# Strassen's algorithm, one level, in the down projection of a ConvGLU layer (20 of 22 contraction tiles), with the weight sums formed in HBM by accumulating DMAs

## The chip, the cores and the metric

The kernel runs on one core of one Trainium2 chip. Work is spread over five engines that run side by side, each with its own queue in a fixed order: TensorE (PE) multiplies matrices into PSUM, VectorE (DVE) and ScalarE (ACT) do elementwise work, GpSimd (POOL) sets memory and issues some DMAs, SyncE (SP) issues most DMAs. They wait for one another through semaphores. All DMAs, whichever queue issues them, share 16 DMA engines. The metric is the device time of one execution in microseconds (us), the median of several runs.

## The reference

One layer: a token mixer, then the channel mixer below, for 512 latent tokens (8 rows of 64), model width 1024, and inner width `D_FF` 2816. Everything is float32. Only the last product is touched by the change.

```python
def _conv_ffn(h, rows, w_up, conv_w, conv_b, w_down):
    bsz, length, _ = h.shape
    a, val = _split(h @ w_up, (D_FF, D_FF))
    img = a.reshape(bsz, rows, length // rows, D_FF)
    a = lax.conv_general_dilated(img, conv_w[:, :, None, :], (1, 1), 'SAME',
                                 dimension_numbers=('NHWC', 'HWIO', 'NHWC'),
                                 feature_group_count=D_FF) + conv_b
    return (jax.nn.gelu(a.reshape(bsz, length, D_FF), approximate=False) * val) @ w_down
...
x = x + g2x * _conv_ffn(hx2, rows, ffn_w_up[l], ffn_conv_w[l], ffn_conv_b[l], ffn_w_down[l])
return _rms_norm(x, final_norm_g)
```

The last product is (512 x 2816) by (2816 x 1024); its result is scaled by `g2x`, added to the residual `x`, and normalised.

## The kernel before

**Numbers as pairs.** A float32 operand goes into TensorE as two float32r tiles, a rounded `hi` and the rest `lo`, and each product is three matmuls: hi·hi, hi·lo, lo·hi. For weights, `stream_split` makes the pair: ACT casts `raw` into `wh` (L185) and DVE subtracts (`wl`, L186). For activations `split_act` does the same (L309, L310).

**The stream of weights.** All weight blocks of 512 KB stand in one list, `specs`, in the order of their use. `weights()` hands out block i, has the blocks up to i + 1 split, and has SP issue the loads up to block i + 3 (`AHEAD`). There are four `raw` buffers and five of `wh` and of `wl`; a load waits until the split of four blocks before has read its buffer. Each block serves 24 matmuls of 512 columns in nearly all stages.

**The order of the work.** A scheduler sets the order of each engine's queue from the program's text and its data dependences; `in_order` pins parts of it. DMAs from SP are issued strictly in queue order, so one that waits holds up all behind it.

**The stages that matter here.** (1) Up to about 245 us: the input products and the linear attention. (2) From there to about 480 us: the spatial gate, the two branch products, and beside them, a few steps per weight block (`tick`), `ada2`: the modulation vector is computed on DVE, with 64 multiply-adds into eight `acc` tiles (L1133) over 64 loads of `w_ada` (tiles `wa`, L1132). In two parts of four, an `acc` tile is first set to zero by POOL (`G.memset`, L1124) and its first row loaded from `b_ada` by SP (L1126). (3) The up projection: 22 tiles `f`, two weight blocks each (L317); `conv_part` does for each the 3x3 convolution as nine taps (ACT L1346, DVE L1352 eight times), Gelu (ACT L1353) and the product with the gate (DVE L1354) into `gact`. (4) The down projection: for each half of the 1024 output columns, 22 contraction tiles, four token tiles of 128 (`down`, L1395): 2 x 22 x 4 x 3 = 528 matmuls. The last `TAIL` = 6 contraction tiles are done token tile by token tile, so that `out_step` and `out_tok` (the scale by g2, the residual, the norm, the store; L1403 to L1427) run beside the rest; the very last tile comes in two pieces of 256 columns.

```python
def down(ps, g, w, kk, t, c0, n, first, last):
    gh, gl_ = g
    wh, wl = w
    for i, (a, b) in enumerate(((gh, wh), (gh, wl), (gl_, wh))):
        T.matmul(ps, a[:, t * P:(t + 1) * P], b[:, kk, c0:c0 + n], start=(first and i == 0),
                 stop=(last and i == 2))
```

**POOL's queue** holds, besides some early constants, 11 small DMAs near 31 us (`rest_load`), two memsets of `pmask`, and the two times four memsets of `acc`.

Of the kernel before, what the change touches and what calls it, by code (L numbers as in the profile page):

```python
# [23 lines left out]
FT = 22  # L24
GW = 64
# [2 lines left out]
HEAP = 44  # L28
LATE = 27
AHEAD = 3  # L30


@with_exitstack
def backbone_kernel(
# [7 lines left out]
    V, A, G, T = nc.vector, nc.scalar, nc.gpsimd, nc.tensor  # L42
# [5 lines left out]
    sp = stack.enter_context(tc.tile_pool(name="sp", bufs=8))  # L48
    pm = stack.enter_context(tc.tile_pool(name="pm", bufs=4, space=bass.MemoryType.PSUM))
    pg = stack.enter_context(tc.tile_pool(name="pg", bufs=4, space=bass.MemoryType.PSUM))  # L50

    cnt = [0]
# [25 lines left out]
    def traced():  # L78
        return nc.cur_bb.bb.instructions

    def in_order(start, *engines):

        last = {}
        for i in traced()[start:]:
            e = i.engine
            if e in engines:
                if e in last:
                    tc.add_manual_dep(i, last[e], mybir.DependencyInfo(
                        mybir.DependencyClass.NoSync, mybir.DependencyReason.DATA), reason="in_order")
                last[e] = i.name  # L90
# [12 lines left out]
    eps_t = const([P, 1], "eps_t")  # L103
# [54 lines left out]
    for f in range(FT):  # L158
        w_cols(ffn_w_up[0], f * P)
        w_cols(ffn_w_up[0], FF + f * P)  # L160
    for half in range(2):
        for k in range(FT // 2):
            w_cols(ffn_w_down[0], half * 512, 512, 2 * k, 2)

    raws, splits = {}, {}
    pos = [0, 0, 0]
# [10 lines left out]
    def stream_split(upto):  # L177
        while pos[1] < min(upto, len(specs)):
            i = pos[1]
            stream_load(i + 1)  # L180
            _, kn, n = specs[i]
            raw = raws.pop(i)
            wh = wp.tile([P, kn, n], F32R, tag="wh", name=nm("wh"))
            wl = wp.tile([P, kn, n], F32R, tag="wl", name=nm("wl"))
            A.copy(wh, raw)  # L185
            V.tensor_tensor(wl, raw, wh.bitcast(F32), op=ALU.subtract)  # L186
            splits[i] = (wh, wl)
            pos[1] += 1
# [117 lines left out]
    def split_act(src, n=512, s="a", lo_pool=heap, hi_pool=heap, eng=None):  # L306
        hi = hi_pool([P, n], F32R, s=s + "h")
        lo = lo_pool([P, n], F32R, s=s + "l")
        (eng or V.tensor_copy)(hi, src)  # L309
        V.tensor_tensor(lo, src, hi.bitcast(F32), op=ALU.subtract)  # L310
        return hi, lo
# [358 lines left out]
    dst, aps = ada_dot(1)  # L670
# [12 lines left out]
    for k in range(1, KT):  # L683
        g = max(i for i in range(NG) if G0[i] <= k)
# [6 lines left out]
        for z in range(3):  # L691
            if nxt and z == AT[g]:
                dst, aps = ada_dot(nxt)
# [41 lines left out]
    for d in range(2):  # L735
        t_ = late([P, 4, P], s="pmask")
# [599 lines left out]
    wide_tm(mg, wo_done, hook, {(2, 6): turn_first})  # L1336


    gact = []
# [31 lines left out]
    stream_split(pos[2] + 2)  # L1371
    in_order(N2[0], T.engine, A.engine, V.engine)
    conv_part(0, pss[0], pss[1])
    for f in range(1, FT):
# [19 lines left out]
        for i, (a, b) in enumerate(((gh, wh), (gh, wl), (gl_, wh))):  # L1394
            T.matmul(ps, a[:, t * P:(t + 1) * P], b[:, kk, c0:c0 + n], start=(first and i == 0),  # L1395
                     stop=(last and i == 2))

    TAIL = 6

    def out_add(pv, hf, t, c0, n):  # L1400
        tmp = late([P, n], s="yt")
        xv = x1[t][hf][:, c0:c0 + n]
        V.tensor_tensor(tmp, pv, bc_g["g2", hf][:, c0:c0 + n], op=ALU.mult)  # L1403
        V.tensor_tensor(xv, xv, tmp, op=ALU.add)
        return tmp, xv

    def out_step(pv, hf, t, c0, n, part):
        tmp, xv = out_add(pv, hf, t, c0, n)
        A.activation(tmp, xv, AF.Square, accum_out=ss3[:, t, part:part + 1])

    def out_tok(t, part, before):

        b_, r = small(1, "n3b"), small(1, "n3r")
        start = len(traced())
        part()
        if before > 1:
            V.reduce_sum(b_, ss3[:, t, :before], axis=AX.X)
            V.tensor_scalar(b_, b_, 1.0 / D, EPS, op0=ALU.mult, op1=ALU.add)
        else:
            V.tensor_scalar(b_, ss3[:, t, 0:1], 1.0 / D, EPS, op0=ALU.mult, op1=ALU.add)  # L1420
        A.activation(r, ss3[:, t, before:before + 1], AF.Sqrt, bias=b_, scale=1.0 / D)
# [4 lines left out]
        V.scalar_tensor_tensor(x1[t][1], x1[t][1], r, fng[1], op0=ALU.mult, op1=ALU.mult)  # L1426
        dma(out[0, t * P:(t + 1) * P, 512:1024], x1[t][1])  # L1427

    for hf in range(2):
        pss = [(mm if hf else gl)() for _ in range(4)]  # L1430
        for kc_ in range((FT - TAIL) // 2):
            w = weights()
            for kk in range(2):
                k = 2 * kc_ + kk
                if hf == 0:
                    gs.append(split_act(gact[k].rearrange("p r w -> p (r w)"), s="g"))
                for t in range(4):
                    down(pss[t], gs[k], w, kk, t, 0, 512, k == 0, hf == 1 and t == 3 and k == FT - TAIL - 1)
        wl3 = [weights() for _ in range(TAIL // 2)]
        if hf == 0:  # L1440
            for k in range(FT - TAIL, FT):
                gs.append(split_act(gact[k].rearrange("p r w -> p (r w)"), s="g", lo_pool=late))
        else:

            out_add(pss[3], 1, 3, 0, 512)
        for t in range(4):
            pieces = [(0, 256), (256, 256)] if hf and t == 3 else [(0, 512)]
            for i, (c0, n) in enumerate(pieces):
                ps = gl() if hf and t == 3 else pss[t]
                for k in range(FT - TAIL, FT):  # L1450
                    down(ps[:, :n], gs[k], wl3[(k - FT + TAIL) // 2], k % 2, t, c0, n,
                         hf == 1 and t == 3 and k == FT - TAIL, k == FT - 1)
                step = lambda: out_step(ps[:, :n], hf, t, c0, n, hf + i)
                if hf == 0 or i + 1 < len(pieces):
                    step()
                else:
                    out_tok(t, step, hf + i)
            if hf == 0:
                xg.append(late([P, 512], s="xg"))
                V.tensor_tensor(xg[t], x1[t][0], fng[0], op=ALU.mult)  # L1460


# [28 lines left out]
```

## Time and profile before

| | |
|---|---|
| median of 3 runs | 939.61 us (939.19 to 940.34) |
| span of the profiled execution | 938.1 us |
| busy: PE, DVE, ACT, POOL | 925.1, 647.5, 365.2, 13.4 us |
| granted TensorE clock, mean | 0.999 |
| bytes read from HBM, written | 109.04 MB, 2.10 MB |

How to read the rows quoted below. The page's first part gives busy time, share of the span and number of instructions for each engine. The chain is the work that ended last, followed back from the end. In timelines and in the chain in order of time, a row begins with its start and its duration in us; neighbouring instructions of one kind are one row with their count. Rows of groups by form end in the busy time in us, the mean of one instruction in ns, and the engine's idle time before them. Rows of stretches (A:B) give for each engine the busy time and the number of instructions, then the clock, the share of time that the 16 DMA engines were busy, and GB/s.

### The profile page before, as it was taken

The numbers are of one execution on the slowest core, as the hardware profiler recorded it, in microseconds if no ns is written. First come the engines' busy times: TensorE is split into PE (matmuls) and PEld (weight loads), VectorE is DVE, ScalarE is ACT, GpSimd is POOL, SyncE is SP. The second block draws the span as 40 slices with busy tenths as digits, with TensorE's granted clock in tenths as the row PEclk, the third lists the DMA queues.
The fourth block names the chain that finished last, engine by engine and source line by source line (L and its number), as shares of the span: only waits on it lengthen the run. The fifth ranks groups of instructions, "written<-read, shape, count | busy, mean of one in ns | idle before, by whom it ended". The sixth has DMA issues, their size and how long they took to land.

```text
span 938.1 us, 12079 instructions
## 1 busy us (share of the span) xinstructions
PE 925.1 (99%) x4618; PEld 773.5 (82%) x4618; DVE 647.5 (69%) x1132; ACT 365.2 (39%) x616; POOL 13.4 (1%) x34
## 2 busy tenths in 40 slices
PE   7999999999999999999999999999999999999997
PEld 5778888888888888888888889888888888888886
DVE  5578687688898652596664358977777777893414
ACT  5356465565542232222222247443333334211313
POOL 1200000000000000000000000000000000000000
PEclk9999999999999999999999999999999999999999
DMA  9951400511508553483532521533333332232302
GB/s 283 320 155 41 118 23 1 180 45 46 158 26 250 175 191 99 139 289 107 185 112 90 188 87 53 155 108 90 101 102 90 91 110 92 81 116 73 113 1 90
DMA packets 146215, 111.93 MB, mean 119 GB/s; under 512 B 5945, under 2 KB 121989, under 8 KB 146157
## 3 DMA queue, kind: packets, MB, share of 16 engines
q1 hardware_dynamic: 145117, 109.85, 37.9%
q10 hardware_dynamic: 688, 1.09, 0.3%
q8 instruction: 36, 0.59, 0.2%
q0 software_dynamic: 352, 0.22, 0.1%
q14 instruction: 22, 0.18, 0.1%
HBM read 109.04 MB, written 2.10 MB: 118 GB/s over the span
## 4 chain that ended last, share of the span: by engine, by line
PE 98%; ACT 0%; DMA 0%; DVE 0%; issue 0%; ACTq 0%
PE mm L317 55%; PE mm L335 12%; PE gl L1395 7%; PE mm L1395 6%; PE gl L841 3%; PE mm L611 2%; PE gl L611 1%; PE mm L948 1%; PE mm L998 1%; PE gl L335 1%; PE gl L520 1%; PE gl L876 1%; PE gl L1164 1%; PE mm L484 1%; PE gl L317 1%; PE mm L328 1%
## 5 line engine op out<-in xcount | busy, mean ns | idle before, releaser
L185 ACT CAST wh<-raw 128x1024 fp32r<-128x1024 f32 x139 | 146.0, 1054 | 356.9 <-PE mm L317 220.4
L186 DVE TENSOR_TENSOR wl<-raw,wh 128x1024 fp32r<-128x1024 f32 x139 | 168.8, 1219 | 125.3 <-ACT wh L185 124.8
L317 PE MATMUL mm<-h2l,wh 128*128 128x512 f32 (+1 forms) x344 | 133.0, 387 | 0.0
L317 PE MATMUL mm<-h2h,wh 128*128 128x512 f32 (+1 forms) x344 | 133.0, 387 | 0.0
L317 PE MATMUL mm<-h2h,wl 128*128 128x512 f32 (+1 forms) x344 | 133.0, 387 | 0.0
L1352 DVE SCALAR_TENSOR_TENSOR cacc<-ca,ccol,cacc 128x441 f32<-128x441 f32 (+2 forms) x176 | 121.8, 695 | 4.4 <-ACT cacc L1346 0.2
L317 PE MATMUL mm<-hxh,wh 128*128 128x512 f32 x296 | 116.1, 392 | 0.0
L317 PE MATMUL mm<-hxl,wh 128*128 128x512 f32 x296 | 115.4, 390 | 0.0
L317 PE MATMUL mm<-hxh,wl 128*128 128x512 f32 x296 | 115.4, 390 | 0.0
L317 PEld LDWEIGHTS mm<-h2l,wh 128*128 128x128 f32 x344 | 64.6, 188 | 13.2
L317 PEld LDWEIGHTS mm<-h2h,wh 128*128 128x128 f32 x344 | 64.6, 188 | 13.2
L317 PEld LDWEIGHTS mm<-h2h,wl 128*128 128x128 f32 x344 | 64.6, 188 | 12.9
L317 PEld LDWEIGHTS mm<-hxh,wl 128*128 128x128 f32 x296 | 55.5, 188 | 11.6
L317 PEld LDWEIGHTS mm<-hxh,wh 128*128 128x128 f32 x296 | 55.6, 188 | 11.2
L317 PEld LDWEIGHTS mm<-hxl,wh 128*128 128x128 f32 x296 | 55.6, 188 | 11.2
L1133 DVE SCALAR_TENSOR_TENSOR acc<-wa,cs,acc 128x512 f32<-128x512 f32 x64 | 45.7, 744 | 1.5 <-DMA wa<-in_w_ada_dram 1.5
L1395 PE MATMUL gl<-wl,gh 128*128 128x512 f32 (+1 forms) x100 | 37.6, 376 | 0.0
L1395 PE MATMUL gl<-wh,gl 128*128 128x512 f32 (+1 forms) x100 | 37.6, 376 | 0.0
L1395 PE MATMUL gl<-wh,gh 128*128 128x512 f32 (+1 forms) x100 | 37.6, 376 | 0.0
L1353 ACT ACTIVATE cacc<-cacc 128x512 f32<-128x512 f32 x22 | 13.9, 632 | 56.6 <-DVE cacc L1352 56.6
L335 PE MATMUL mm<-wh,hxh 128*128 128x512 f32 x88 | 34.7, 394 | 0.0
L335 PE MATMUL mm<-wl,hxh 128*128 128x512 f32 x88 | 34.4, 390 | 0.0
(398 smaller groups left out, 1671.6 us busy)
## 6 DMA issues: line engine op xcount, KB each, us to landing
raw<-in_w_in_dram SPq DMA_DIRECT2D x52, 512.0 KB, 3.8
wa<-in_w_ada_dram SPq DMA_DIRECT2D x96, 256.0 KB, 4.6
raw<-in_ffn_w_up_dram SPq DMA_DIRECT2D x44, 512.0 KB, 3.7
raw<-in_ffn_w_down_dram SPq DMA_DIRECT2D x22, 512.0 KB, 3.5
raw<-in_w_br_a_dram SPq DMA_DIRECT2D x8, 512.0 KB, 5.2
raw<-in_w_br_b_dram SPq DMA_DIRECT2D x8, 512.0 KB, 3.9
raw<-in_w_o_dram SPq DMA_DIRECT2D x8, 512.0 KB, 3.6
xin<-in_x_dram SPq DMA_DIRECT2D x8, 256.0 KB, 3.4
```

The lines of the kernel that those rows point to most:

```text
L185: A.copy(wh, raw)
L186: V.tensor_tensor(wl, raw, wh.bitcast(F32), op=ALU.subtract)
L317: T.matmul(ps, a[:, k, :], b[:, c0:c0 + n], start=(k == 0 and i == 0), stop=(k == KT - 1 and i == 2))
L328: T.matmul(ps, a[:, k, :], b[:, c0:c0 + n], start=(k == 0 and i == 0), stop=(k == KT - 1 and i == 2))
L335: T.matmul(ps, a[:, t * P:(t + 1) * P], b[:, k % 2, :], start=(k == 0 and i == 0), stop=(k == KT - 1 and i == 2))
L484: T.matmul(xps[1][:, :256], ones, ident.unsqueeze(1).to_broadcast([P, 2, P]), start=True, stop=True)
L611: T.matmul(fps[i], a, b, start=(k == 0 and z == 0), stop=(k == KT - 1 and z == 2))
L841: T.matmul(ps, p_, q_, start=(start and z == 0), stop=(stop and z == 2))
L1133: V.scalar_tensor_tensor(acc[j], w_, cs[:, k, 0:1], acc[j], op0=ALU.mult, op1=ALU.add)
L1352: V.scalar_tensor_tensor(o, a_[:, r0 + dy:r1 + dy, c0 + dx:c1 + dx], wcol(tap), o, op0=ALU.mult, op1=ALU.add)
L1353: A.activation(acc, acc, AF.Gelu)
L1395: T.matmul(ps, a[:, t * P:(t + 1) * P], b[:, kk, c0:c0 + n], start=(first and i == 0), stop=(last and i == 2))
```

## The change

**The products.** Tiles 0 to 19 of the contraction are taken in five blocks (`BLOCKS`) of four. In each block the activations are a 2 x 2 matrix (token halves of 256, pairs of contraction tiles) and so are the weights (pairs of contraction tiles, output halves of 512). A form of Strassen's scheme with seven products computes the 2 x 2 result. A product over one block is 2 token tiles x 2 contraction tiles x 3 = 12 matmuls; one product over all five blocks adds up in two PSUM banks (`products`). So 7 x 5 x 12 = 420 matmuls stand for 480; tiles 20 and 21 stay as they were (48 matmuls, `rest_in`).

**The results.** DVE joins the seven products with adds and subtracts of 128 x 512 (`combine`, results in `u2`, `w5`, `u4`, `c21`, `e22`), partly out of PSUM; ACT takes the first one out (`taken`). The second output half is partly added to the residual early (`todo`).

**The activations.** `conv_part` writes the product with the gate as two halves of 256 tokens into `gpair`. `all_preps` forms for each of the 35 (product, block) pairs its operand, a quarter or a sum or difference of quarters (`tile_op`, 128 x 512 on DVE), and splits it (`act_both`: ACT `dah`, DVE `dal`). Up to eight (`EARLY`) are made during the up projection, later ones five (`LEAD`) ahead of use.

**The weights.** Four of the seven weight operands are sums of quarters. They are formed in HBM: 20 tiles `sum` of 256 x 512 (rows padded to 576), by 20 plain copies and 20 DMAs that add to what stands there (`accum_op`), all on POOL's queue. One is issued at each call of `weights()` from the third block on; each waits for the instruction that was written last before it. The 40 DMAs span blocks 2 to 41 of the stream. The down projection then takes 37 blocks of 512 KB from the stream instead of 22: 20 of them are `sum` tiles, and each of the 35 product blocks serves 12 matmuls.

**The end.** The order at the end is new: in the second output half, three blocks of the last product, then token tiles 2 and 3 by their rest alone, then for token tiles 0 and 1 the last two blocks and the rest. The last tile is no longer cut in two pieces. A dummy square root on ACT stands ahead of the end.

On POOL's queue the eight memsets of `acc` used to follow the memsets of `pmask` directly (before):

```order
L737 MEMSET pmask_951 128x512
L1124 MEMSET acc_2913 128x512
L1124 MEMSET acc_2916 128x512
L1124 MEMSET acc_2919 128x512
L1124 MEMSET acc_2922 128x512
L1124 MEMSET acc_3957 128x512
```

Now 17 sum DMAs stand ahead of the first four and 39 ahead of the last four; these are the rows around the last four (the change; L192 are copies, L194 accumulating DMAs, L1164 the memsets):

```order
L194 DMA sum_121<-sum_120 256x512
L194 DMA sum_117<-sum_116 256x512
L194 DMA sum_125<-sum_124 256x512
L194 DMA sum_129<-sum_128 256x512
L1164 MEMSET acc_4018 128x512
L1164 MEMSET acc_4021 128x512
L1164 MEMSET acc_4024 128x512
L1164 MEMSET acc_4027 128x512
L194 DMA sum_133<-sum_132 256x512
```

The memsets have moved behind the issue of these DMAs. On SP's queue nothing has moved there; the loads of `b_ada` into `acc` still stand ahead of eight loads of `wa` and of the next weight block (rows of the change):

```order
L1166 DMA acc_2961<-in_b_ada_dram 1x512
L1172 DMA wa_647_2964<-in_w_ada_dram 128x512
L1172 DMA wa_648_2967<-in_w_ada_dram 128x512
...
L1172 DMA wa_694_3188<-in_w_ada_dram 128x512
L1172 DMA wa_695_3191<-in_w_ada_dram 128x512
L211 DMA raw_3317<-in_w_br_a_dram 128x8x128
```

In the middle of the down projection DVE used to have splits of weights, one in 24 matmuls, and the results of the first half (before, `yt` and `x` of L1403 and L1404):

```order
L186 TENSOR_TENSOR wl_7674<-raw_7517,wh_7673 128x1024
L186 TENSOR_TENSOR wl_7704<-raw_7647,wh_7703 128x1024
L1403 TENSOR_TENSOR yt_7633<-gl_7196,g_995_4820 128x512
L186 TENSOR_TENSOR wl_7734<-raw_7677,wh_7733 128x1024
L1404 TENSOR_TENSOR x_1034_5023<-x_1034_5023,yt_7633 128x512
```

The change puts there, for each 12 matmuls, a split of weights (`wl`), a split of an activation operand (`dal`), often a sum (`ds`), and the joins (`dc`):

```order
L224 TENSOR_TENSOR wl_7705<-raw_7652,wh_7704 128x1024
L1426 TENSOR_TENSOR dal_7773<-ds_7770,dah_7772 128x512
L1431 TENSOR_TENSOR ds_7800<-gp_6917,gp_6918 128x512
L224 TENSOR_TENSOR wl_7729<-raw_7684,wh_7728 128x1024
L1557 TENSOR_TENSOR dc_7666<-dt_7435,mm_7554 128x512
L1557 TENSOR_TENSOR dc_7668<-dt_7437,mm_7555 128x512
L1557 TENSOR_TENSOR dc_7670<-gl_7439,dc_7666 128x512
L1557 TENSOR_TENSOR dc_7672<-gl_7440,dc_7668 128x512
L224 TENSOR_TENSOR wl_7753<-raw_7708,wh_7752 128x1024
L1426 TENSOR_TENSOR dal_7803<-ds_7800,dah_7802 128x512
```

The diff, cut to its core:

```diff
+BLOCKS = 5
+TAIL = FT - 4 * BLOCKS
+LEAD = 5
+EARLY = 8
...
+    quarter = lambda b, row, col: ffn_w_down[0][(4 * b + 2 * row) * P:(4 * b + 2 * row + 2) * P,
+                                                 col * 512:(col + 1) * 512]
+    sums = [[dp.tile([2 * P, 576], F32, name=nm("sum"))[:, :512] for _ in range(4)]
+            for _ in range(BLOCKS)]
...
+    def sums_build():
+        for step in (((0, (0, 1)), (1, (1, 1)), (2, (1, 0)), (3, (0, 1))), ((0, (0, 0)), (3, (1, 1))),
+                     ((1, 0),), ((2, 1),)):
+            for b in range(BLOCKS):
+                for dst, src in step:
+                    ap = quarter(b, *src) if isinstance(src, tuple) else sums[b][src]
+                    after = traced()[-1]
...
+                    if len(step) == 4:
+                        G.dma_start(sums[b][dst], ap)
+                    else:
+                        G.dma_start(sums[b][dst], ap, accum_op=ALU.add)
...
     def weights():
         i = pos[2]
         pos[2] += 1
+        if i > 1:
+            next(building, None)
         stream_split(i + 2)
...
-        V.tensor_tensor(acc, acc, pv.rearrange("p (r w) -> p r w", w=GW), op=ALU.mult)
-        gact.append(acc)
+        if f < 4 * BLOCKS:
+            if f % 2 == 0:
+                gpair.append([heap([P, 2, 256], s="gp") for _ in range(2)])
+            for hf in range(2):
+                V.tensor_tensor(gpair[-1][hf][:, f % 2, :],
+                                acc[:, 4 * hf:4 * hf + 4, :].rearrange("p r w -> p (r w)"),
+                                pv[:, hf * 256:(hf + 1) * 256], op=ALU.mult)
...
+    def act_both(src, pool=heap):
+        hi = pool([P, 2, 256], F32R, s="dah")
+        lo = pool([P, 2, 256], F32R, s="dal")
+        A.copy(hi, src)
+        V.tensor_tensor(lo, src, hi.bitcast(F32), op=ALU.subtract)
+        return hi, lo
...
+        prep(min(EARLY, BLOCKS, (f + 1) // 4) if f < 4 * BLOCKS - 2 else min(EARLY, f - 4 * BLOCKS + 3 + BLOCKS))
...
+    def products(bank, blocks=BLOCKS, stop=True):
+        banks = [bank() for _ in range(2)]
+        for b in range(blocks):
+            z = operands()
+            for t in range(2):
+                product_in(banks[t], t, 0, 512, z, b == 0, stop and b == blocks - 1)
+            if todo:
+                todo.pop(0)()
+        return banks
...
+    m1 = [taken(z) for z in products(gl)]
+    m5 = products(gl)
+    m6 = products(mm)
+    u2 = [combine(m, z, ALU.add) for z, m in zip(m6, m1)]
+    w5 = [combine(z, u, ALU.subtract) for z, u in zip(m5, u2)]
+    m4 = products(mm)
+    u4 = [combine(u, z, ALU.add) for u, z in zip(u2, m4)]
+    m7 = products(gl)
+    c21 = [combine(u, z, ALU.add) for u, z in zip(u4, m7)]
+    e22 = [combine(w, z, ALU.subtract) for w, z in zip(w5, m7)]
+    for t in range(4):
+        todo.append(lambda t=t: out_add((w5 + e22)[t], 1, t, 0, 512))
...
+    acc = products(gl, stop=False)
...
+    for t in range(4):
+        ps = acc[t] if t < 2 else mm()
+        rest_in(ps, t, 0, 512, w, t > 1)
+        e = (m1 + c21)[t]
+        V.tensor_tensor(e, ps, e, op=ALU.add)
+        out_step(e, 0, t, 0, 512, 0)
...
+    acc = products(mm, first, False)
+    zs = [operands() for _ in range(BLOCKS - first)]
+    w = [weights() for _ in range(TAIL // 2)]
+    for t in (2, 3):
+        ps = gl()
+        rest_in(ps, t, 0, 512, w, True)
+        out_tok(t, lambda: out_step(ps, 1, t, 0, 512, 1), 1)
+    for t in range(2):
+        for z in zs:
+            product_in(acc[t], t, 0, 512, z, False, False)
+        rest_in(acc[t], t, 0, 512, w, False)
+        out_tok(t, lambda: out_step(acc[t], 1, t, 0, 512, 1), 1)
```

More of the change, by code (lines that the diff above doesn't have):

```diff
@@ L50, in backbone_kernel @@
     pg = stack.enter_context(tc.tile_pool(name="pg", bufs=4, space=bass.MemoryType.PSUM))
+    dp = stack.enter_context(tc.tile_pool(name="dp", bufs=1, space=bass.MemoryType.DRAM))
     cnt = [0]
@@ L1336, in backbone_kernel @@
     wide_tm(mg, wo_done, hook, {(2, 6): turn_first})
-    gact = []
+    gact, gpair = [], []
     def conv_part(f, pa, pv):
@@ L1353, in conv_part @@
         A.activation(acc, acc, AF.Gelu)
-        V.tensor_tensor(acc, acc, pv.rearrange("p (r w) -> p r w", w=GW), op=ALU.mult)
-        gact.append(acc)
+        if f < 4 * BLOCKS:
[5 more added lines that the diff above has]
+                                pv[:, hf * 256:(hf + 1) * 256], op=ALU.mult)
+        else:
+            V.tensor_tensor(acc, acc, pv.rearrange("p (r w) -> p r w", w=GW), op=ALU.mult)
+            gact.append(acc)
     ws = [splits.pop(pos[2] + i) for i in range(2)]
@@ L1396, in down @@
                      stop=(last and i == 2))
-    TAIL = 6
     def out_add(pv, hf, t, c0, n):
@@ L1427, in out_tok @@
         dma(out[0, t * P:(t + 1) * P, 512:1024], x1[t][1])
[L1429 to L1460, printed above, removed]
@@ new lines, in backbone_kernel, with product_in, operands @@
+    n, todo = [0], []
+    def product_in(ps, t, c0, n_, z, first, last):
+        (wh, wl), (ah, al) = z
+        for kk in range(2):
+            c = kk * 256 + t * P
+            hi, lo = (y.rearrange("p k t -> p (k t)")[:, c:c + P] for y in (ah, al))
+            for i, (a, w) in enumerate(((hi, wh), (hi, wl), (lo, wh))):
+                T.matmul(ps, a, w[:, kk, c0:c0 + n_], start=(first and kk == 0 and i == 0),
+                         stop=(last and kk == 1 and i == 2))
+    def operands():
+        prep(n[0] + LEAD)
+        z = weights(), ready[n[0]]
+        ready[n[0]] = None
+        n[0] += 1
+        return z
@@ new lines, in products, with combine, taken @@
+    def products(bank, blocks=BLOCKS, stop=True):
[7 more added lines that the diff above has]
+        return banks
+    def combine(a, b, op):
+        t_ = late([P, 512], s="dc")
+        V.tensor_tensor(t_, a, b, op=op)
+        return t_
+    def taken(ps):
+        t_ = late([P, 512], s="dt")
+        A.copy(t_, ps)
+        return t_
@@ new lines, in rest_in @@
+    def rest_in(ps, t, c0, n_, w, first):
+        for k in range(TAIL):
+            down(ps, gs[k], w[k // 2], k % 2, t, c0, n_, first and k == 0, k == TAIL - 1)
+    acc = products(gl, stop=False)
+    w = [weights() for _ in range(TAIL // 2)]
+    start = len(traced())
+    for g_ in gact:
+        gs.append(split_act(g_.rearrange("p r w -> p (r w)"), s="g", lo_pool=late, eng=A.copy))
+    A.activation(small(1, "root"), eps_t, AF.Sqrt)
+    in_order(start, A.engine)
+    for t in range(4):
[4 more added lines that the diff above has]
+        out_step(e, 0, t, 0, 512, 0)
+        xg.append(late([P, 512], s="xg"))
+        V.tensor_tensor(xg[t], x1[t][0], fng[0], op=ALU.mult)
@@ new lines, in backbone_kernel @@
+    first = BLOCKS - 2
+    acc = products(mm, first, False)
+    zs = [operands() for _ in range(BLOCKS - first)]
+    w = [weights() for _ in range(TAIL // 2)]
+    for t in (2, 3):
[7 more added lines that the diff above has]
+        out_tok(t, lambda: out_step(acc[t], 1, t, 0, 512, 1), 1)
```

58 lines of the change are left out of this document (55 added, 3 removed).

## The prediction

> **What bounds the kernel now.** I read the page first, then the chain in order of time, then stretches, forms and timelines.
>
> ```profile
> span 938.1 us, 12079 instructions
> PE 925.1 (99%) x4618; PEld 773.5 (82%) x4618; DVE 647.5 (69%) x1132; ACT 365.2 (39%) x616; POOL 13.4 (1%) x34
> PE 98%; ACT 0%; DMA 0%; DVE 0%; issue 0%; ACTq 0%
> 811.74 59.84 PE gl L1395 x264
> 871.58 55.76 PE mm L1395 x246
> 927.34 4.32 PE gl L1395 x36
> 931.68 0.44 DVE yt L1403
> 932.14 0.44 DVE x L1404
> 932.60 0.27 ACT yt L1409
> 933.67 0.75 DVE x L1426
> ```
>
> TensorE is the chain, 98% of it. The down projection takes it from 811.74 to 931.66 us without a gap: 59.84 / 264 = 0.2267 us per matmul of 512 columns, and 4.32 / 36 = 0.12 us for the 36 halves of the last tile. What follows, 6.4 us to the end of the span, is the last tile's scale, residual, norm and store. A change that takes matmuls out of this stage shortens the end one for one, as long as no other engine falls behind. So the question is what DVE, the DMAs and POOL have left:
>
> ```profile
> 730.00:780.00 50.00, 50.00 (x222) 41.42 (x221) 39.12 (x51) 18.82 (x24) 0.00 (x0) 1.00 0.34 99
> 820.00:840.00 20.00, 20.00 (x90) 16.57 (x89) 19.73 (x37) 4.19 (x4) 0.00 (x0) 1.00 0.38 129
> 840.00:860.00 20.00, 20.00 (x90) 16.57 (x89) 6.61 (x7) 3.19 (x4) 0.00 (x0) 1.00 0.28 95
> ```
>
> DVE (the third number with a count) is 78% busy in the up projection and, after the activation splits end near 840, a third or less.
>
> **Step 1, matmuls: -13.6 us.** 528 become 420 + 48 = 468. 60 x 0.2267 = 13.6 us, all on the chain.
>
> **Step 2, the end: +0.9 us.** The last tile is no longer cut, so the scale, the residual add and the square run on 512 columns.
>
> ```profile
> L1404 DVE TENSOR_TENSOR x<-x,yt 128x512 f32<-128x512 f32 x8 | 5.5, 692 | 0.2
> L1409 ACT ACTIVATE yt<-x 128x512 f32<-128x512 f32 x7 | 4.4, 632 | 28.5 <-DVE x L1404 28.5
> ```
>
> 0.69 + 0.69 + 0.63 against 0.44 + 0.44 + 0.27 in the chain: 0.86 us. The rest of the end is unchanged.
>
> **Step 3, DVE and ACT in the down projection: 0, hidden, but narrowly.**
>
> ```profile
> L186 DVE TENSOR_TENSOR wl<-raw,wh 128x1024 fp32r<-128x1024 f32 x64 | 77.9, 1221 | 62.5 <-ACT wh L185 62.5
> L310 DVE TENSOR_TENSOR gl<-cacc,gh 128x512 fp32r<-128x512 f32 x22 | 14.9, 686 | 0.3
> 819.01 0.68 DVE L310 TENSOR_TENSOR gl<-cacc,gh 128x512 fp32r<-128x512 f32 x1
> 819.61 0.42 DVE L309 CAST gh<-cacc 128x512 fp32r<-128x512 f32 x1
> 819.95 1.22 DVE L186 TENSOR_TENSOR wl<-raw,wh 128x1024 fp32r<-128x1024 f32 x1
> 821.08 0.68 DVE L310 TENSOR_TENSOR gl<-cacc,gh 128x512 fp32r<-128x512 f32 x1
> L185 ACT CAST wh<-raw 128x1024 fp32r<-128x1024 f32 x64 | 67.3, 1056 | 144.9 <-PE mm L317 84.5 <-PE gl L1395 30.3 <-PE mm L1395 21.9
> ```
>
> After the last gate of the up projection DVE's queue has 30 weight splits, 81 operations of 128 x 512 (26 `dal`, 11 `ds`, 14 joins, 28 of the residual and the gain, 2 `gl`) and 4 at the very end of 0.75. By durations: 30 x 1.22 + 81 x 0.69 + 3 + 1 for small ones = 97 us. The stage's matmuls take 468 x 0.2267 = 106 us. Independent neighbours start closer together than they last (819.01 to 819.61 is 0.60, 819.95 to 821.08 is 1.13), which gives 30 x 1.13 + 81 x 0.61 + 4 = 87 us. So DVE is between 82% and 92% full. It is not even: one product is 60 matmuls, 13.6 us; by durations the fourth needs 5 x 1.22 + 14 x 0.69 = 15.8, the fifth 6.1 + 7 x 0.69 = 10.9, the last of the first output half 6.1 + 22 x 0.69 = 21.3. The overhang of 7.3 us in these three (48.1 against 40.8) is what must be worked off ahead; operands are made 5 blocks ahead (5 x 2.72 = 13.6 us) and the first three products need less than they take (10.2, 9.6, 9.6). I cost it at nothing; without that lead it is 7.3 us. ACT needs 1.06 + about 0.6 of each 2.72 us and has room.
>
> In the up projection a tile takes 10.9 us and DVE has 22% of it free, 2.4 us. The gate in two halves adds 2 x 0.43 - 0.69 = 0.17, an operand 0.69, and the last three with a difference and an update 3 x 0.69 = 2.07: all under 2.4, so 0.
>
> ```profile
> L1300 DVE TENSOR_TENSOR h2l<-h2f,h2h 128x256 fp32r<-128x256 f32 x16 | 6.6, 425 | 0.7
> ```
>
> **Step 4, the stream in the down projection: 0.** 37 loads instead of 22, one of 512 KB per 12 matmuls, 2.72 us: 193 GB/s.
>
> ```profile
> raw<-in_ffn_w_down_dram SPq DMA_DIRECT2D x22, 512.0 KB, 3.5
> 280.00:308.00 28.00, 28.00 (x149) 24.07 (x148) 25.36 (x36) 7.73 (x11) 0.00 (x0) 1.00 0.80 251
> 308.00:350.00 42.00, 42.00 (x187) 34.76 (x186) 24.83 (x32) 13.37 (x16) 2.11 (x4) 1.00 0.53 171
> 280.00:400.00 120.00, 120.00 (x554) 99.98 (x553) 71.54 (x93) 34.50 (x43) 2.11 (x4) 1.00 0.55 170
> ```
>
> TensorE stayed full (busy as long as the stretch) at 171 GB/s, the engines 0.53 busy, and at 251, 0.80 busy; a load lands in 3.5 us and is asked for three blocks, 8 us, ahead.
>
> **Step 5, forming the sums: +2 us, the least certain.** 40 DMAs of 0.52 MB join the traffic between about 100 and 395 us. By the rows above the engines carry about 171 / 0.53 = 320 GB/s when full, so a copy takes 1.6 us of all 16 engines. No row shows an accumulating DMA; from below it is one pass (1.6), and two passes (it reads two tiles) are 3.2. Twelve of the twenty are issued between 308 and 350, by the DVE instructions they wait for (the second of them for the first row here, the ninth for the second):
>
> ```profile
> 310.05 2.07 DVE L1133 SCALAR_TENSOR_TENSOR acc<-wa,cs,acc 128x512 f32<-128x512 f32 x3
> 344.13 0.69 DVE L310 TENSOR_TENSOR accl<-acc,acch 128x512 fp32r<-128x512 f32 x1
> ```
>
> At one pass that is 12 x 1.6 = 19 us on top of 0.53 x 42 = 22, and just fits in 42; at two 38 + 22 = 60, which does not. But nobody reads a sum before 811 us, so the sums can be late; the loads have their lead. The Trainium skill speaks against this change here: in Collectives: The Full Stack, section "The bandwidth ceiling: the fold count and why AG ≠ RS ≠ AR", an add in a DMA costs two source reads on one ring, half the rate of a copy. No run here shows it yet; by it the two-pass figure would hold.
>
> The other path is POOL's queue, since SP waits for its memsets.
>
> ```profile
> 33.49 1.48 POOL L264 DMA_DIRECT2D w2r<-in_gla_w_dram  x3
> 245.15 1.92 POOL L1124 MEMSET acc<- 128x512 f32 x4 [194.98 <-ACT junk L928]
> 248.48 1.35 SPq L1126 DMA_DIRECT2D acc<-in_b_ada_dram  x4
> 249.94 8.00 SPq L1132 DMA_DIRECT2D wa<-in_w_ada_dram  x8
> 279.76 0.38 SPq L173 DMA_DIRECT2D raw<-in_w_br_a_dram  x1
> 249.31 8.30 DVE L1094 TENSOR_SCALAR vsn<-vr,mv,var 128x128 f32<-128x128 f32 x32
> 266.25 1.41 DVE L1133 SCALAR_TENSOR_TENSOR acc<-wa,cs,acc 128x512 f32<-128x512 f32 x2
> wa<-in_w_ada_dram SPq DMA_DIRECT2D x16, 256.0 KB, 4.5
> 382.71 0.68 DVE L1153 TENSOR_REDUCE col_sh<-dg 128x4 f32<-128x512 f32 x1
> 383.24 1.31 SPq L1126 DMA_DIRECT2D acc<-in_b_ada_dram  x4
> ```
>
> The 17th sum DMA waits for the last of the 32 `vsn` (ends 257.6). Behind it the first memsets move from 245.15 to about 258.5 (0.5 us to issue, by 1.48 / 3), SP's `b_ada` to 259 to 261, the first `wa` lands 4.5 us later near 266: just in time for DVE at 266.25. SP's next weight load is due at 279.76, and the eight `wa` take 8 us from 261, so the stream is not touched. The 39th waits for the `col_sh` that ends at 383.4, so the last memsets come 1 to 3 us after SP wants them at 383.24. Bounds for step 5: 0, if all of it is hidden, and about 10 if the loads bear the overlap (below). I take 2, near the lower end, because the loads are early and the sums may wait.
>
> **Sum.** -13.6 + 0.9 + 2 = -10.7. The profiled span goes from 938.1 to 927.4; the median of the runs lies 1.5 above that span, so **928.9 us**.
>
> **Rivals.** (a) DVE becomes the bound in the down projection. For it: 92% by durations, two of the last three products of the first half over their time. Against: the lead. Price 7.3 us: 936.2. (b) Traffic: with two passes and the engines shared turn by turn, the loads get half. Between 280 and 308 they want 0.80 of the engines, 28 x 0.30 = 8 us late, and some more up to 350, less their lead: 0 to 10, say 5 more than my 2: 934. (c) Slower: POOL's queue jams. Eight semaphores go round, so the 39th sum DMA also waits until the 31st has landed. From 280 to 400 the loads use 55% of the engines; the sums get 45%. At four passes (6.4 us) 8 accumulates are through by 400, and the 31st, the eleventh of them, lands near 420, 35 us after SP wants the memsets; behind them stand the `wa` loads and the next weight load. With two blocks of lead, 2 x 24 x 0.2267 = 11 us, TensorE loses some 20 us: 928.9 + 20 = 949. It decides above three passes (5 us): then the memsets come after about 405, and more than 11 us are lost. Against it: one small POOL DMA lands in 5.8 us, latency included.
>
> ```profile
> w2r<-in_gla_w_dram POOLq DMA_DIRECT2D x6, 32.0 KB, 5.8
> ```
>
> **Chances.** My forecast 0.50 (926 to 932), (a) 0.13, (b) 0.15, (c) 0.22. The measurement can tell 0.2%, 1.9 us: faster means under 937.7. All of the forecast, most of (a) and (b): 0.74; within 0.2% the rest of these, 0.05; slower 0.21. The range 925.5 (steps 3 to 5 all hidden, and 1 us less at the end) to 939 holds the forecast, (a) and (b): 0.8.
>
> **What would show it.** Right: 468 matmuls at 0.227 in the down projection with no gap, DVE 80 to 95% there, memsets of `acc` near 258 and 385, TensorE full from 280 to 420. Step 3 wrong: gaps of TensorE that end with `wl` or `dal`. Step 5 wrong: gaps between 280 and 420 that end with `wh` or `acch`, `wa` landing in over 6 us, or `acc` memsets long after 385.

## The result, and the profile after

The changed kernel takes 930.47 us (median, 929.44 to 932.99), beside 939.45 us for the kernel before on the same chip: a ratio of 0.9906, 95% interval 0.9891 to 0.9921, or 9.0 us less. The prediction was 928.9 us. The profiled execution took 931.05 us, 1.75 more than its span of 929.3.

The page after, its span, engines and chain:

```profile
span 929.3 us, 12172 instructions
PE 913.0 (98%) x4540; PEld 761.3 (82%) x4540; DVE 690.7 (74%) x1197; ACT 400.8 (43%) x669; POOL 42.3 (5%) x74
PE 85%; DMA 6%; DVE 4%; SPq 3%; ACT 1%; issue 1%; DVEq 0%; ACTq 0%
```

TensorE was 98% of the chain; now 13% of it leads over DMAs, DVE and SP. Where that is, the chain in order of time tells (start, duration, what). First a stretch in the middle, then the down projection:

```profile
348.11 8.79 DMA wa<-in_w_ada_dram
...
357.78 0.63 ACT acch L349
...
362.81 16.31 DMA raw<-in_w_in_dram
...
380.28 0.02 issue
380.31 0.41 DVE wl L224
...
384.51 0.51 PE gl L1181
385.01 7.09 PE mm L357 x31
...
811.87 4.08 PE mm L357 x18
815.95 27.20 PE gl L1535 x120
843.15 27.20 PE mm L1535 x120
...
920.67 1.37 PE mm L1495 x6
922.04 0.02 issue
922.06 0.70 DVE yt L1501
```

The down projection has no gap: 922.04 - 815.95 = 106.1 us where it was 931.66 - 811.74 = 119.9. But it begins 4.2 us later, and the end behind the last matmul takes 929.3 - 922.04 = 7.3 us where it was 6.4. So the span's change of -8.8 us is -13.8 in the stage, +0.8 at the end, and +4.2 ahead of the stage.

The 4.2 us can be placed by setting the same TensorE instruction of both traces side by side. The change begins in the first 20 us, before any sum DMA is issued: 0.5 us there. The profiled executions of the experiments below are, at 20 us, from 1.2 earlier to 0.9 later than the kernel before, so that part is the spread of starts. Then come 0.7 us near 261, 0.9 near 357 and 2.0 near 381, with 0.1 spread over the rest. Behind 385 nothing more is lost. The stretches, with busy time of each engine, clock, DMA share and GB/s:

```profile
280.00:400.00 120.00, 118.03 (x541) 97.38 (x540) 67.99 (x89) 32.52 (x41) 19.01 (x24) 1.00 1.01 243
350.00:400.00 50.00, 48.03 (x208) 38.53 (x207) 23.30 (x30) 14.24 (x19) 9.32 (x13) 1.00 1.02 238
```

The DMA engines, 0.55 busy between 280 and 400 us before, are now full. The DMAs issued between 280 and 420 us (size, median us from issue to landing), of the kernel before and then of the changed one:

```profile
wa<-in_w_ada_dram SPq DMA_DIRECT2D x46, 256.0 KB, 4.6
raw<-in_w_in_dram SPq DMA_DIRECT2D x18, 512.0 KB, 3.8
```

```profile
wa<-in_w_ada_dram SPq DMA_DIRECT2D x46, 256.0 KB, 6.8
raw<-in_w_in_dram SPq DMA_DIRECT2D x17, 512.0 KB, 8.2
sum<-in_ffn_w_down_dram POOLq DMA_DIRECT2D x10, 512.0 KB, 8.2
sum<-sum POOLq DMA_DIRECT2D x10, 512.0 KB, 8.4
```

And the group of multiply-adds of `ada2` on DVE after (the last column is idle time before them, and for what):

```profile
L1173 DVE SCALAR_TENSOR_TENSOR acc<-wa,cs,acc 128x512 f32<-128x512 f32 x64 | 46.0, 744 | 34.7 <-DMA wa<-in_w_ada_dram 34.6
```

DVE stands at these for 34.6 us (1.5 before). The weight splits stand behind them in DVE's queue, and SP asks for the next load when a split has freed a buffer. So in the chain above a `wa` load of 8.8 us leads to the loss at 357, and a weight load of 16.3 us to the one at 381. That load was asked for in the middle of a bunch of sum DMAs. POOL issued six of them between 358.7 and 368.2, four of which are these:

```profile
358.70 1.78 POOL L194 DMA_DIRECT2D sum<-sum  x2 [11.00 <-DVE acc L1173]
361.34 1.78 POOL L194 DMA_DIRECT2D sum<-sum  x2 [0.85 <-DVE acc L1173]
```

Each sum DMA waits for the instruction written last before it, here multiply-adds of DVE. When DVE has stood at a `wa`, several become due at once.

The 0.7 us near 261 are something else. DVE and POOL there, after:

```profile
259.19 1.83 DVE L1143 TENSOR_SCALAR o<-o,var 128x256 f32<-128x256 f32 x1
260.94 0.67 DVE L350 TENSOR_TENSOR swl<-swT,swh 128x512 fp32r<-128x512 f32 x1
```

```profile
258.37 0.56 POOL L192 DMA_DIRECT2D sum<-in_ffn_w_down_dram  x1 [32.55 <-DVE vsn L1134]
258.92 1.96 POOL L1164 MEMSET acc<- 128x512 f32 x4
```

and DVE before:

```profile
258.73 0.35 DVE L1103 TENSOR_SCALAR o<-o,var 128x256 f32<-128x256 f32 x1
```

The memsets, moved behind a sum DMA, now run while DVE scales `o`: one operation of 0.35 us takes 1.83 and ends as the memsets end (260.88), and the split `swl`, on which TensorE waits, comes later. The Trainium skill, in SBUF — State Buffer, section "Who interferes with whom", says that GpSimd shares a pair of ports with some DVE operations by a lock, that a `tensor_scalar` can be one of these, and that the second to issue is blocked until the first is done. This trace agrees that `o`, which began 0.27 us after the memsets, was held, by 1.48 us; but it was held until the last of four memsets, not of one.

### The profile page after: what moved, and what is told of

It is laid out like the page before. It is cut to its first block, busy times and chain, and to the rows that moved or that the text cites. A ratio compares the mean times of both kernels' runs of the same rounds, so it can differ in the third digit from the quotient of the medians.

```text
span 929.3 us, 12172 instructions
## 1 busy us (share of the span) xinstructions
PE 913.0 (98%) x4540; PEld 761.3 (82%) x4540; DVE 690.7 (74%) x1197; ACT 400.8 (43%) x669; POOL 42.3 (5%) x74
## 4 chain that ended last, share of the span: by engine, by line
PE 85%; DMA 6%; DVE 4%; SPq 3%; ACT 1%; issue 1%; DVEq 0%; ACTq 0%
PE mm L357 48%; PE mm L375 11%; PE gl L1535 6%; PE mm L1535 4%; DMA wa<-in_w_ada_dram 3%; PE gl L881 3%; DMA raw<-in_w_in_dram 2%; SPq L273 1%; PE mm L988 1%; PE mm L1038 1%; PE mm L651 1%; PE gl L375 1%; DVE wl L224 1%; DVE vsn L1134 1%; SPq L294 1%; PE gl L916 1%
## 5 line engine op out<-in xcount | busy, mean ns | idle before, releaser
L223 ACT CAST wh<-raw 128x1024 fp32r<-128x1024 f32 x154 | 161.7, 1054 | 316.0 <-PE mm L357 180.9
L224 DVE TENSOR_TENSOR wl<-raw,wh 128x1024 fp32r<-128x1024 f32 x154 | 186.8, 1219 | 73.7 <-ACT wh L223 73.1
L1173 DVE SCALAR_TENSOR_TENSOR acc<-wa,cs,acc 128x512 f32<-128x512 f32 x64 | 46.0, 744 | 34.7 <-DMA wa<-in_w_ada_dram 34.6
L375 PE MATMUL mm<-wh,hxl 128*128 128x512 f32 x88 | 34.3, 390 | 0.0
L1535 PE MATMUL gl<-wl,dah 128*128 128x512 f32 x80 | 31.1, 389 | 0.0
L1535 PE MATMUL gl<-wh,dah 128*128 128x512 f32 x80 | 31.1, 389 | 0.0
```

The lines of the kernel that those rows point to most:

```text
L1173: V.scalar_tensor_tensor(acc[j], w_, cs[:, k, 0:1], acc[j], op0=ALU.mult, op1=ALU.add)
L1535: T.matmul(ps, a, w[:, kk, c0:c0 + n_], start=(first and kk == 0 and i == 0), stop=(last and kk == 1 and i == 2))
```

## The experiments

Theory A: the stage brings its 13.8 us whole, and what is missing is the sums' traffic between 280 and 400 us, with a small part from the moved memsets. Rivals: the new work beside the up projection costs it; POOL's queue order costs it; an accumulate as such does; DVE is near its limit.

**No sums.** The down projection reads raw quarters.

```diff
-        by_block(lambda b: sums[b][i])
+        by_block(lambda b: quarter(b, *((0, 1), (1, 1), (1, 0), (0, 1))[i]))
...
-        if i > 1:
-            next(building, None)
```

> Leaves out the 40 sum DMAs; the down projection loads raw quarters in place of the sums, so its loads, matmuls, DVE and ACT work are unchanged. Theory A (the sums' traffic between 280 and 400 us, and with it the late wa and weight loads, cost about 2.9 us, the memsets moved behind a sum DMA 0.7 us): 930.5 - 3.6 = 926.9, between 926 and 928; the down projection starts near 812 instead of 815.95 us, DVE waits for wa a few us in all, not 34.7. Rival B (the 4.2 us come from the new work itself, the gate in halves and the operands beside the up projection, not from the sums): 930 to 931, the start stays near 816.

Measured: 926.95 us (926.24 to 927.97), and the engines' share is as it was before the change:

```profile
280.00:400.00 120.00, 120.00 (x554) 100.03 (x553) 71.80 (x92) 34.37 (x43) 2.11 (x4) 1.00 0.55 169
```

DVE waits for `wa` for 0.6 us. Theory A holds: all that the sums cost is 930.47 - 926.95 = 3.5 us; the new work beside the up projection costs nothing, and between 20 us and the down projection TensorE loses nothing against the kernel before.

**Copies in place of accumulates.**

```diff
-                        G.dma_start(sums[b][dst], ap, accum_op=ALU.add)
+                        G.dma_start(sums[b][dst], ap)
```

> The 20 accumulating DMAs become plain copies in the same places of POOL's queue, so the adding is left out. Theory A with an accumulate worth two passes of the DMA engines: 20 x 1.6 = 32 us of engine time less between 280 and 400 us, the engines fall from a share of 1.0 to about 0.8, DVE's wait for wa from 34.7 to under 15 us, the time to about 928 (927.3 to 929). Rival C (an accumulate costs the engines no more than a copy): no change, 930 to 931, and wa as late as before.

Measured: 926.97 us (926.77 to 927.80); no gap near 357 or 381.

```profile
280.00:400.00 120.00, 120.00 (x554) 100.03 (x553) 71.67 (x93) 34.41 (x43) 13.09 (x24) 1.00 0.80 253
```

DVE waits for `wa` for 9.0 us. 40 copies cost next to nothing; rival C falls. The memsets stand here where the change has them, and they hold `o` as there:

```profile
257.94 1.84 DVE L1143 TENSOR_SCALAR o<-o,var 128x256 f32<-128x256 f32 x1
```

TensorE loses 0.8 us near 261 and nothing else, so this loss doesn't depend on the adding. A copy's price: (0.80 - 0.55) x 120 us = 30 us of all engines for (253 - 169) x 120 us / 0.524 MB = 19.2 copies, 1.56 us each, as the prediction had it.

**The memsets first.** No sum is issued in the two calls ahead of them.

```diff
-        if i > 1:
+        if i > 1 and i not in (18, 40):
             next(building, None)
```

> The same 40 sum DMAs, but none is issued in the two calls that stand ahead of the memsets of acc, so both groups of memsets stand ahead of the sum DMA that held them up. Theory A: the 0.7 us near 261 come back (DVE's o tile is not held for 1.5 us by the memsets), the rest stays: 929.8, within 929 and 930.6. Rival D (the loss is POOL's queue: memsets late, SP held up at b_ada, the loads behind it late): 3 to 4 us come back, 926.5 to 927.5.

Measured: 928.84 us (926.46 to 931.71): the spread is too wide to tell the two theories apart by time. The trace does it: DVE's scaling of `o` is short again and nothing is lost near 261,

```profile
257.73 0.36 DVE L1143 TENSOR_SCALAR o<-o,var 128x256 f32<-128x256 f32 x1
```

while DVE waits for `wa` for 38.2 us and TensorE still loses 0.7 us near 357 and 2.1 near 381. So the memsets were the small part, and the queue's order is not the large one.

**The sums late.** The same sums, 24 of the 40 DMAs moved into the up projection.

```diff
-        if i > 1:
+        if 1 < i < 18 or i > 57 and i % 5 in (0, 2, 4):
             next(building, None)
```

> The same sums, but only 16 copies are issued early (calls 2 to 17); the other 4 copies and the 20 accumulates are issued 3 in 5 calls from call 59 to 97, in the up projection, where the engines' share is 0.33 to 0.42. Theory A: nothing is late between 240 and 400 us and the down projection starts near 812: 927 (926 to 928), faster than the changed kernel by 3.5 us. Rival E (the sums now hold up the up projection's loads, or the first sum tiles come too late for the down projection): 930 or more, with gaps of PE that end with wh or wl between 480 and 830 us.

Measured: 926.38 us (926.14 to 926.84), ratio to the kernel before 0.9863 (0.9847 to 0.9879); the down projection begins at 811.17. The stretch from 480 to 800 us, of the kernel before and of the late one:

```profile
480.00:800.00 320.00, 320.00 (x1474) 267.19 (x1474) 230.39 (x328) 121.76 (x174) 0.00 (x0) 1.00 0.34 104
```

```profile
480.00:800.00 320.00, 320.00 (x1475) 267.31 (x1474) 237.63 (x358) 125.86 (x181) 19.93 (x24) 1.00 0.57 142
```

TensorE stays full. The price of an accumulate can be read here: (0.57 - 0.34) x 320 = 73.6 us of all engines, less 4 copies of 1.56, over 20: 3.4 us, 2.2 times a copy. By the Trainium skill, Collectives: The Full Stack, section "The bandwidth ceiling: the fold count and why AG ≠ RS ≠ AR", in a ring ReduceScatter runs at about half the rate of AllGather, because its add needs two source reads where a copy needs one. The price here agrees in size; its cause no run here shows.

Both kernels once more, on one chip:

> The changed kernel once more, beside the late kernel on one chip, to size what the place of the sums costs. Both theories of the loss: 930 to 931, with a spread of some us, since the loads there have no lead left.

> The late kernel once more: 926.4 (925.8 to 927.2), 4 us under the changed kernel, spread under 1 us.

Measured: 930.30 us (928.95 to 930.84; ratio 0.9905, 0.9888 to 0.9921) and 926.87 us (926.29 to 927.11; ratio 0.9865, 0.9851 to 0.9880). The place of the sums costs 3.4 us. In the profiled execution of the changed kernel (928.95 us) TensorE loses 0.7 us near 261 and 1.9 near 381, but nothing near 357, so that loss does not come in every execution.

**The sums at half the rate.**

```diff
-        if i > 1:
+        if 1 < i < 18 or i > 18 and i % 2:
             next(building, None)
```

> The same 40 sum DMAs: 16 copies in calls 2 to 17 as in the changed kernel, then one in every second call up to call 65, where the changed kernel has one in every call up to 41. With an accumulate at 3.4 us of the 16 engines (the late kernel: a share of 0.57 against 0.34 over 320 us, 74 us for 20 accumulates and 4 copies at 1.56), one per 10.9 us adds 0.31 to a mean share of 0.55: theory A says it fits, 926.5 to 927.3, with DVE waiting for wa under 12 us. Rival G (any accumulate beside the wa loads makes DVE late, whatever the rate): 928.5 or more, with DVE waiting for wa over 25 us.

Measured: 927.01 us (925.72 to 927.82), with a share of 0.78 from 280 to 400 us, 9.9 us of DVE's waits for `wa`, and TensorE full. Accumulates beside the `wa` loads do no harm as long as the engines have room; rival G falls.

**Two copies for each accumulate.**

```diff
+    spare = [dp.tile([2 * P, 576], F32, name=nm("spare"))[:, :512] for _ in range(20)]
...
-                        G.dma_start(sums[b][dst], ap, accum_op=ALU.add)
+                        G.dma_start(sums[b][dst], ap)
+                        G.dma_start(spare.pop(), ap)
```

> Each accumulate of the changed kernel becomes two plain copies (the second to a spare tile), in the same place; the adding is left out. Theory A (it is the engines' time, and an accumulate is worth about two copies: 2 x 1.56 = 3.1 against 3.4 us): the loss comes back, a share near 0.97 between 280 and 400 us, DVE waiting for wa over 20 us, 929 to 930.5. Rival F (an accumulate has something that two copies have not, such as its latency or an order it forces): as with one copy, 927 to 927.8.

Measured: 947.41 us (946.41 to 947.60), 17 us over the changed kernel, and outside both expectations. The loads between 280 and 420 us land still later than with accumulates:

```profile
wa<-in_w_ada_dram SPq DMA_DIRECT2D x35, 256.0 KB, 8.3
raw<-in_w_in_dram SPq DMA_DIRECT2D x15, 512.0 KB, 9.9
```

The way is the same as in the changed kernel, by a `wa` load at 357 and a weight load at 374 (chain, then stretches, then a wait of TensorE):

```profile
357.15 9.54 DMA wa<-in_w_ada_dram
...
369.76 4.56 PE mm L360 x15
...
374.34 21.09 DMA raw<-in_w_in_dram
```

```profile
350.00:400.00 50.00, 36.49 (x137) 28.17 (x136) 21.69 (x28) 11.62 (x16) 9.51 (x18) 0.86 0.94 295
368.00:380.00 12.00, 11.76 (x42) 9.21 (x43) 9.25 (x12) 7.16 (x11) 6.62 (x12) 0.81 0.93 292
```

```profile
PE gl L1183 <- ACT acch L352: 9.6, 2, 6.0
```

TensorE stands for 13.5 of the 50 us from 350 to 400. Its longest wait is 6.0 us (the last row: total, times, longest), and after such waits it is granted a slower clock, 0.81 from 368 to 380: 15 matmuls take 4.56 us, 0.30 each. The down projection begins at 832.41, 20.7 us later than before. Without the waits 7.2 us are left; matmuls that follow one another without a wait account for about 5 of them, so the slow clock costs 5 to 7 us. Rival F, that an accumulate has something harmful of its own, falls in the other direction: two copies do more harm than it. Theory A has the path right (late `wa`, then a late weight load) and missed the size. The loss is not in proportion to the traffic. It would be what exceeds the lead of the loads, which the changed kernel had used up; this is argued, not shown. Why an accumulate with 3.4 us of engine time delays the loads less than two copies with 3.1 was not settled; it writes half as many bytes. The bunches are one candidate that was not tested apart: POOL issued ten copies between 368.5 and 375.5 us, by the price above 10 x 1.56 = 16 us of all engines, and the weight load of 21.1 us was asked for among them.

**DVE's lead shortened**, on the late kernel.

```diff
-LEAD = 5
-EARLY = 8
+LEAD = 1
+EARLY = 5
```

> The late kernel with operands made 1 block ahead (LEAD 5 to 1) and 5 instead of 8 in the up projection (EARLY); the same work. If DVE is as full in the down projection as the prediction said, the overhang of the last products of the first output half, up to 7.3 us, now shows as gaps of PE that end with dal, wl or a join: 930 (928 to 933.5). Rival H (DVE has room to spare, the lead is idle): 926 to 927, no gaps.

Measured: 926.37 us (925.58 to 926.69), no gap of TensorE in the stage. `LEAD` orders the program's text, and DVE runs ahead of TensorE all the same. One operand of this run, as DVE makes it and as TensorE first uses it (the tenth, counted in order):

```profile
827.97 0.68 DVE L1426 TENSOR_TENSOR dal<-ds,dah 128x512 fp32r<-128x512 f32 x1
835.93 0.39 PE L1535 MATMUL gl<-wh,dal 128*128 128x512 f32 x1
```

It is ready 7.3 us ahead. From there to the end of the first output half the operands are ready 7.3 to 16.4 us ahead, in the late kernel 15.5 to 27.3. So the lead was shortened, not taken away: half of it is enough, and what would happen without it this run doesn't show.

**DVE loaded further**, on the late kernel: one operation more in 33 of the 35 product blocks (the last two are taken outside `products`, where the line stands).

```diff
+    spare = const([P, 512], "spare")
...
             z = operands()
+            V.tensor_tensor(spare, fng[0], fng[1], op=ALU.mult)
```

> The late kernel with one more DVE operation of 128 x 512 in each of the 35 product blocks, with an unused result: it sizes the room that DVE has in the down projection. If DVE counts by durations as in the prediction (97 + 35 x 0.69 = 121 us against 106 of matmuls): 15 us longer less what is worked off ahead, 934 to 941. If it counts by the distance of starts (87 + 35 x 0.61 = 108): 927 to 930.

Measured: 935.72 us (935.40 to 936.95), 9.1 us over the late kernel (926.63 over its 8 runs). DVE is full, and TensorE waits, mostly between 880 and 900 us, for `wl` of DVE (2.4 us) and for `gh` of ACT (2.7):

```profile
860.00:900.00 40.00, 36.18 (x156) 29.03 (x155) 40.00 (x57) 21.07 (x27) 0.00 (x0) 0.98 0.49 158
```

33 x 0.61 = 20.1 us were added by the distance of starts, and 20.1 - 9.1 = 11.0 of them absorbed: DVE had room for about 18 more operations of 128 x 512. The time lies in the range of the count by durations (934 to 941), but that count isn't borne out: in this run too the starts of neighbours of 0.68 us are 0.60 apart. The count by starts began from 87 us, and DVE is busy for 95.6 us of the late kernel's stage (why, see step 3 below). From there it gives 95.6 + 20.1 - 106.1 = 9.6 us, against 9.1 measured.

**`wa` asked for earlier**, the changed kernel with its sums in place; `wa_load(k)` issues the four loads of a row block.

```diff
-            for k in range(KT):
+            def wa_load(k):
...
-                    V.scalar_tensor_tensor(acc[j], w_, cs[:, k, 0:1], acc[j], op0=ALU.mult, op1=ALU.add)
...
+            ahead = wa_load(0)
+            for k in range(KT):
+                now, ahead = ahead, wa_load(k + 1) if k + 1 < KT else None
+                for j in range(4):
+                    V.scalar_tensor_tensor(acc[j], now[j], cs[:, k, 0:1], acc[j], op0=ALU.mult, op1=ALU.add)
```

> The changed kernel, sums in their place, but the four wa loads of a row block are asked for before the multiply-adds of the block ahead of it. If the loss goes by way of DVE (its queue stands at a multiply-add that waits for wa, and the weight splits and so the next loads stand behind it): DVE's wait for wa falls below 15 us and the time to 927 to 928.5, although the engines stay full. Rival J (the weight loads themselves land too late, whatever DVE waits for): 929.5 to 931.

Measured: 930.23 us (930.06 to 930.96). DVE's wait for `wa` fell from 34.6 to 23.0 us only, so the condition of the first expectation (below 15) was not reached, and the loss moved: TensorE is full from 350 to 400 and loses 1.7 us from 308 to 350, in waits for `ah` and `al` of DVE:

```profile
308.00:350.00 42.00, 40.26 (x174) 32.28 (x173) 23.81 (x32) 13.10 (x16) 7.04 (x8) 1.00 1.05 260
```

This doesn't separate DVE's queue from the weight loads' own lateness; which of the two carries more stays open. With the engines full, asking earlier only moves the place.

**The last tile cut in two**, on the late kernel.

```diff
...
+    product_in(acc[1], 1, 0, 512, zs[0], False, True)
+    out_add(acc[1], 1, 1, 0, 512)
+    for i in range(2):
+        ps = gl()[:, :256]
+        product_in(ps, 1, i * 256, 256, zs[1], True, False)
+        rest_in(ps, 1, i * 256, 256, w, False)
...
```

> The late kernel with the last token tile's last block and rest in two pieces of 256 columns, what stands before added to the residual early: the scale, the add and the square at the very end work on 256 columns. By the prediction's step 2, 0.86 us less at the end, and 36 matmuls of 256 columns at 0.12 for 18 of 512 at 0.2267 add 0.24: 926.4 - 0.6 = 925.8 (925.4 to 926.2). Rival I (the end is set by the stores, or the early piece comes in the way): 926.4 or more.

Measured: 926.22 us (925.79 to 926.76), the lowest of all, 0.2 and 0.65 us under the two medians of the late kernel: just outside the expected 925.4 to 926.2 and under rival I's 926.4. The runs of the two kernels overlap, so by time nothing is settled. In the trace the span ends 6.6 us after TensorE's last matmul, 7.3 in the late kernel.

## Why the prediction came out as it did

- **What bounds the kernel, and step 1 (-13.6): right.** The stage went from 119.9 to 106.1 us, -13.8; the 0.2 more is that the last tile's 36 halves at 0.12 us became 18 whole matmuls at 0.2267.
- **Step 2 (+0.9): right.** 0.8 in the trace.
- **Step 3 (0, hidden but narrowly): right in the result, half right in the reasons.** DVE is busy for 95.5 of the stage's 106.1 us, 90%, near the upper end of the 82 to 92% that the step gave (stretch, then DVE's last product with the gate, after):

```profile
815.95:922.04 106.09, 106.08 (x468) 87.49 (x467) 95.51 (x130) 60.04 (x86) 0.00 (x0) 1.00 0.51 156
823.94 0.68 DVE L1402 TENSOR_TENSOR cacc<-cacc,mm 128x512 f32<-128x512 f32 x1
```

  The agreement with the upper end is in part luck. The step's list begins behind the last gate, and that stands 8.0 us into the stage; until then DVE works without a pause on twelve operations that the list lacks (the last tile's taps and gate, three splits, three sums and splits of operands). The count by starts, 87 us, plus these 8 comes to 95; counting by durations, which overlap, made up for the missing ones. That the lead hides an overhang of 7.3 us is neither shown nor refuted: with `LEAD` at 1 the time is the same, but the operands were still ready 7.3 us ahead or more. Over the fifth product that lead falls from 16.4 to 9.7 us and then recovers, so something is worked off there. Rival (a) did not occur.
- **Step 4 (0): right.** No gap in the stage.
- **Step 5 (+2): the term that was mis-sized; it measured 3.4 to 3.5.** With that in the sum the prediction is 928.9 + 1.5 = 930.4. The step left open whether an accumulate is one pass (1.6) or two (3.2); it is two (3.4 measured, and 1.56 for a copy). Right too was its reckoning that at two passes 60 us of engine time do not fit into the 42 from 308 to 350. The sentence that failed is "But nobody reads a sum before 811 us, so the sums can be late; the loads have their lead." The sums did not give way: they shared, and the loads became late (3.8 to 8.2 us). And the lead is not all there is, since `wa`, for which DVE's queue stands, has little of it; by that way the splits fell up to 13.6 us behind (361.57 for 348.00 us), and the load behind that split came too late at 381. How much DVE's queue and how much the weight loads' own lateness carries was not separated. This is rival (b)'s mechanism at 1.5 us over the forecast, not the 5 that it gave.
- **Step 5, POOL's queue: right in its times, and one cost not seen.** The first memsets stood at 258.92 (258.5 predicted), the last at 388.32 (385). The path that was looked at, `wa` just in time for DVE, held. What was not looked at was what DVE does while the memsets run: 0.7 us of the 3.5. In all five traces in which the memsets run near 258 us (the changed kernel twice, the plain copies, the two copies, `wa` earlier) `o` takes 1.82 to 1.84 us and TensorE loses 0.7 to 0.8; in those in which they run near 245 it loses nothing there. Rival (c), a jam from three passes (5 us) on, did not occur; an accumulate takes 3.4.

## What to carry to other kernels

A transfer that nobody waits for is not free: here it did not yield to those that somebody waits for. Place it where the share of the DMA engines leaves room for its whole price (here 3.4 us of all engines for each 512 KB added in HBM), and count the lead of the shortest-lived load beside it, not of the best-prefetched one. The same 40 DMAs cost 3.4 us in one place and nothing in another: the late kernel takes 926.4 to 926.9 us.

## What was not expected of the hardware

- A POOL memset can hold a DVE operation: 0.35 us became 1.83, until the last of four memsets was through. In the kernel before, DVE ran splits and copies beside the same memsets at 245 us and none was held; no scaling of `o` stood there.
- Long gaps of TensorE cost a second time. In the changed kernel, with waits of 1.1 us at most, the clock stayed at 1.00. With waits of up to 6.0 us it averaged 0.86 over 50 us, and 5 to 7 of the 20.7 us that TensorE fell behind were the slow clock. Where between these lengths the clock gives way was not measured.
- The busy share of the DMA engines does not rank the harm: at 1.01 from 280 to 400 us (accumulates) the weight loads landed in 8.2 us, at 0.95 (two copies) in 9.9.
